# Two groups of products cut at 432 and 256 columns, and a modulation shift summed on TensorE for every feature tile

## The chip, the cores and the metric

The kernel runs on one core of one Trainium2 chip. The metric is the time of one execution on the device, in microseconds (us). Engines are named PE (TensorE, the matrix engine; PEld is its loading of weights), DVE (VectorE), ACT (ScalarE), POOL (GpSimd) and SP (SyncE, whose queue issues the transfers).

## The reference

The reference is a transformer of two layers over 512 latent tokens (`x`) and 256 context tokens (`ctx`) of 1024 features, in float32. Only the beginning of layer 0 matters here. A conditioning vector, one for the latents and one for the context, is passed through silu and multiplied by `ada_w`, which gives six modulation parts; the first two are a shift and a scale:

```
m_lat = split(silu(c) @ ada_w[l] + ada_b[l], 6)
m_ctx = split(silu(c_ctx) @ ada_w[l] + ada_b[l], 6)
u_lat = x * (1 + m_lat[1]) + m_lat[0]
u_ctx = h * (1 + m_ctx[1]) + m_ctx[0]
p_lat, p_ctx = u_lat @ w_in, u_ctx @ w_in
```

The columns of `w_in` are queries, keys, values and gates of a gated linear attention (4 heads with values of 128) and queries, keys and values of a windowed attention. Behind the mixers come an output projection, LayerNorm and an MLP, and then the second layer with a recurrent mixer and a latent attention.

## The kernel before

All 768 tokens stay on the chip. Activations lie as [feature in tile, feature tile, token], with 8 feature tiles of 128. To keep float32 accuracy, each operand of the large products is split into a high and a low part (`split`: ACT casts, DVE subtracts), and each product is made in three passes (high x high, high x low, low x high).

The part around the change is the first 170 us:

1. `ada_first` makes silu of the conditioning, and spreads it over all partitions (`scb`).
2. `in0` is a generator: each step loads, for one feature tile, the weights of the scale (`scraw`, 512 KB, three buffers), those of the shift (`shraw`, 512 KB, two buffers) and the tile of tokens (`x`, 384 KB, three buffers), in this order on the SP queue. It sums scale and shift for both streams, adds the bias, and makes the activation on ACT (`u` at L450 and its high part `acthi` at L451), and the low part `actlo` on DVE (L452). The scale is always summed on DVE by `ada_dot` (L391: weights times the spread activation, summed along the free axis). The shift is summed on PE for the tiles named in `SHP` (0, 1, 3, 5, 7; L440, eight products of two columns into PSUM), and by `ada_dot` for tiles 2, 4 and 6.
3. `proj_moving(0, ...)` takes those tiles as they come: with 128 tokens stationary, it multiplies by `VM` = 344 columns of weights (L472 to L474), for 6 token tiles and 8 feature tiles, into six PSUM banks. Its weights (`wraw`) come two feature tiles at a time, 2 x 344 columns. `ev0` copies out the gate inputs (48 columns), the values of the windowed attention (128) and the first part of the values `vt` of the gated heads (168).
4. Nine blocks of outputs are then projected with weights stationary (`dense`, L343 to L347), in parts of 512 and 256 tokens. Beside them DVE makes further modulation parts (`ada_chunk`, `araw`, L391 again); for keys and queries of the windowed attention there is a rotation by position (`rp` at L918 on PE, L920 to L922 on DVE).
5. `proj_moving(1, ...)` makes the other 344 columns, all of them `vt`, copied by `ev1`. Then come the output gates, and the gated heads, whose first product on PE is `z` at L507.

The order of the instructions of each engine is written by a scheduler, which takes what is ready by its own model of the durations, first by program order (or a priority given by `prio`), so work of later steps can fill gaps of earlier ones. On the chip, each engine and the SP queue go through this order as written.

Of the kernel before, what the change touches and what calls it, by code (L numbers as in the profile page):

```python
# [16 lines left out]
P = 128  # L17
# [33 lines left out]
SHP = (0, 1, 3, 5, 7)  # L51
PARTS = ((0, 512), (512, 256))
GH = 4
VM = 344
# [9 lines left out]
def _blocks(w):  # L64
    """[K, M] -> [M/128, 128 (k in tile), K/128, 128 (m in block)]"""
    k, m = w.shape
    return np.ascontiguousarray(w.reshape(k // P, P, m // P, P).transpose(2, 1, 0, 3))
# [18 lines left out]
def _rope_perm(half, reps):  # L86
    """lhsT of the signed swap: out[j] = sum_p m[p, j] x[p]; x1 rows get -x2, x2 rows get x1."""
    nf = half // 2
    d = 2 * half
    m = np.zeros((d * reps, d * reps), np.float32)  # L90
    for r in range(reps):
        for b in (0, half):
            for i in range(nf):
                a, c = r * d + b + i, r * d + b + nf + i
                m[c, a] = -1.0
                m[a, c] = 1.0
    return m


class Pack:  # L100
    """columns of one [128, n] array, found by name"""
# [16 lines left out]
def prepare(i):  # L118
# [19 lines left out]
    # shape-only constants  # L138
# [20 lines left out]
    # modulation weights  # L159
    aw = i['ada_w']  # L160
    def outer(w):
        """[D, D] -> [128 (output in tile), tile, inner dimension]"""
        return w.reshape(D, KT, P).transpose(2, 1, 0)
    sh = [outer(aw[0][:, :D])[:, k] if k not in SHP else _blocks(aw[0][:, k * P:(k + 1) * P])[0].reshape(P, D) for k in range(KT)]
    a['ada_sh'] = np.ascontiguousarray(np.stack(sh))
# [3 lines left out]
    # layer 0 mixer  # L169
# [6 lines left out]
    a['w0_m'] = np.ascontiguousarray(mv.reshape(KT, P, 2, VM).transpose(2, 1, 0, 3))  # L176
    a['w0_o'] = _blocks(i['ab_w_out'][0])
    # layer 1 mixer
# [54 lines left out]
def blocks(*ws):  # L233
    """the weights of each block of outputs, from parts of the inner dimension"""
    return [tuple(w[d].rearrange("p k m -> p (k m)") for w in ws) for d in range(KT)]


class Act:
    """activations [128, KT, tokens], a tile for each part of the tokens; a slice of the tokens lies in one part"""
# [17 lines left out]
class Build:  # L257
# [6 lines left out]
    @contextmanager  # L264
    def prio(self, d):
        """what is issued inside stands d instructions later (earlier, if negative) in the scheduler's order"""
# [36 lines left out]
    def psum(self, b, s=0, **more):  # L303
        """PSUM as b single banks and s pairs of banks; more: banks of other tags. Tiles of a tag start in program
        order, so streams that run side by side have tags of their own"""
# [14 lines left out]
    def split(self, raw, hi, lo, eng=None):  # L320
        """raw = hi + lo exactly, both as float32r"""
# [3 lines left out]
    def weights(self, src, n=1024, keep=None, lead=PW):  # L325
        """one [128, n] block of weights from DRAM (or two halves of one), split"""
# [12 lines left out]
    def mm3(self, whi, wlo, ahi, alo, first, last, outs):  # L339
        """outs: list of (psum, slice of the moving operand); one k tile in three passes"""  # L340
# [8 lines left out]
    def dense(self, whi, wlo, hi, lo, nk, parts=PARTS):  # L349
        """[128 out, tokens] += w^T act; w [128, nk*128]; returns one psum tile per part"""  # L350
# [9 lines left out]
    def ada_first(self, pool, m0):  # L360
        """silu of the conditioning on all partitions, [128, stream, inner dimension]"""
# [25 lines left out]
    def ada_dot(self, pool, raw, ws, out):  # L387
        """out(w) = the weights [128, inner dimension] times the activation of stream w; raw is overwritten"""
# [4 lines left out]
    def ada_chunk(self, pool, l, j, among=False):  # L393
        """modulation part j of layer l, a tile of 128 outputs at a time: the weights with the inner dimension on
        the free axis, multiplied by the activation on all partitions and summed"""
# [26 lines left out]
    def in0(self, m0, hi, lo):  # L422
        """x * (1 + scale) + shift, split, tile after tile of the features"""
# [5 lines left out]
        for k in range(KT):  # L429
# [7 lines left out]
            if k in SHP:  # L437
                sh = self.bank("sh", "n")[:, 0:2]
                for q in range(KT):
                    nc.tensor.matmul(sh, rb[:, q * P:(q + 1) * P], self.sc[:, q], start=(q == 0), stop=(q == KT - 1))  # L440
            self.ada_dot(m0, ra, (0, 1), lambda w: m[:, 1, w:w + 1])
            if k not in SHP:
                self.ada_dot(m0, rb, (0, 1), lambda w: m[:, 0, w:w + 1])
                sh = m[:, 0]
# [10 lines left out]
    def proj_moving(self, g, hi, lo, evac, feed=None):  # L455
        """[tokens, VM] = u w with the tokens stationary; feed: makes the tiles of u one after the other"""
        nc = self.nc
        outs = [self.bank("mv") for _ in range(TT)]
        for k2 in range(KT // 2):
            for _ in range(FEED if feed and k2 == 0 else 0):  # L460
                next(feed, None)
            whi, wlo = self.weights(self.a['w0_m'][g, :, 2 * k2:2 * k2 + 2].rearrange("p k m -> p (k m)"), 2 * VM,
                                    lead=0 if feed else PW)
            for kk in range(2):
# [3 lines left out]
                wh, wl = whi[:, kk * VM:(kk + 1) * VM], wlo[:, kk * VM:(kk + 1) * VM]  # L468
                for t in range(TT):
                    uh, ul = hi[:, k, t * P:(t + 1) * P], lo[:, k, t * P:(t + 1) * P]  # L470
                    o = outs[t][:, :VM]
# [3 lines left out]
        for t in range(TT):  # L475
            evac(t, outs[t][:, :VM])

    def sigmoid(self, out, src, tmp):
        """1 / (1 + exp(-src)), all on ACT within one table set"""
# [5 lines left out]
    def gla_setup(self, m0):  # L485
        """operands of each level of halved blocks, with zeros where a side has none"""
# [11 lines left out]
    def gla_head(self, m0, mx_, h, qd, kd, vt, a1T, g):  # L498
        """decays, decayed queries and keys, chunk states of one head, into g[h]"""
        nc = self.nc  # L500
        HALF = (slice(0, 64), slice(64, 128))
        # log decays (times 16): rows 0-63 forward, rows 64-127 backward shifted by one token
# [25 lines left out]
        # exponents of the middles of the chunks  # L528
# [16 lines left out]
        # state contributions of each chunk  # L545
# [25 lines left out]
    def gla_levels(self, cs, lev, W, wm, qd, kd):  # L571
        """operands of the pairs within the chunks cs, by halving blocks; a level's products two levels behind
        its exponentials"""
# [27 lines left out]
        def second(b, Dt):  # L601
# [4 lines left out]
            if b == 1:  # L606
                # neighbours and the token itself (twice, once for each direction)
# [23 lines left out]
    def gla_window(self, m0, h, cs, lev, qt, vh, S, og, hi, lo):  # L631
        """outputs of the chunks cs from the level operands and the states; normed, gated, split"""
# [48 lines left out]
    def gla(self, m0, setup, g, qd, kd, og, hi, lo):  # L681
        """all heads, in windows of two chunks: levels of the next window beside the products of this one. Those of the first are there"""
# [28 lines left out]
    def gqa(self, m0, mx_, queries, KS, K2, vg, hi, lo):  # L711
        """grouped-query attention, head by head. The scores with the queries on the partitions give each query's
        maximum; it is three more rows (exact bfloat16 parts) of the product with the keys on the partitions. The
        queries are [hi; lo] over 128 partitions against [hi; hi] of the keys, then hi against lo. Columns of
        ones beside the values give the sums, and the sink's weight is added to those."""
# [135 lines left out]
    def mixer0(self):  # L851
# [3 lines left out]
        with tc.tile_pool(name="m0", bufs=1, side="right", reuse_waits="tile") as m0, ExitStack() as m0_, \  # L855
# [15 lines left out]
            def ev0(t, o):  # L871
                nc.scalar.copy(at[:, t], o[:, 0:48])
                nc.scalar.copy(vg[:, t, 1::2], o[:, 48:176].rearrange("p (i d) -> p i d", i=2))
                nc.scalar.copy(vt[:, t, 0:VM - 176], o[:, 176:VM])

            def ev1(t, o):
                nc.scalar.copy(vt[:, t, VM - 176:512], o)
# [3 lines left out]
            with tc.tile_pool(name="ma", bufs=1, reuse_waits="tile") as ma:  # L881
# [27 lines left out]
                # grouped-query attention projections, with rope on the latent tokens  # L909
# [25 lines left out]
            # gates of the GLA heads, and the decays of the first one  # L935
# [27 lines left out]
            with tc.tile_pool(name="mb", bufs=1, reuse_waits="tile") as mb:  # L963
# [11 lines left out]
                def queries(i):  # L975
                    """parts of two heads' queries: [hi; lo] of the even head, [lo; hi] of the odd one"""
# [16 lines left out]
    def project(self, ws, hi, lo, z, g, l, parts, sums, norm, keep=None, kept=(), lead=PW):  # L993
        """z += gate * (w^T act), one part of the tokens after the other; sums collects z over the blocks. The
        norm of a part runs beside the products of the next; returns that of the last part. ws: for each block,
# [1034 lines left out]
```

## Time and profile before

| | |
|---|---|
| median of 3 runs | 2121.8 us (2116.98 to 2125.74) |
| span of the profiled execution, first to last instruction | 2106.9 us |
| PE busy | 1976.5 us, 94% |
| DVE busy | 1391.4 us, 66% |
| ACT busy | 952.7 us, 45% |
| POOL busy | 308.6 us, 15% |

The runs time the whole execution, the span only what lies between the first and the last instruction; no time of the profiled execution other than its span is given. Busy shares are means over stages with different limits; matmuls are pipelined, so that PE's busy time overlaps itself.

### The profile page before, as it was taken

Reading aid. Unit: us, or ns where it says so; the run is one execution under the profiler, and the core shown is the slowest. Engines: PE = TensorE matmul, PEld = TensorE weight load, DVE = VectorE, ACT = ScalarE, POOL = GpSimd, SP = SyncE. Lnnn points to the kernel's source line nnn. Section 1 sums busy time; section 2 is a strip of 40 time slices with the busy share of each in tenths; the row PEclk is TensorE's granted clock in tenths of the full one; section 3 lists DMA queues with packets and bytes.
Section 4 is the critical chain, followed back from the end, with each engine's and each line's share of the span. In section 5 each row is a group of like instructions: output and inputs, shape, how many; then the busy total and the mean of one; then the engine's idle time right before and its main releaser. Section 6 shows DMA issues by size and latency. Waiting matters only on the chain. (4 is left out here: it accounts for less than half of the span.)

```text
span 2106.9 us, 35640 instructions
## 1 busy us (share of the span) xinstructions
PE 1976.5 (94%) x14304; PEld 1643.3 (78%) x14304; DVE 1391.4 (66%) x2574; ACT 952.7 (45%) x1835; POOL 308.6 (15%) x517
## 2 busy tenths in 40 slices
PE   8998999989899999999989999978888899999998
PEld 6877666667788888888878877767677797888887
DVE  8775898736897656534484558878887555444454
ACT  5426676544622222222255646765654535333332
POOL 0003455301200000000021020033342011000001
PEclk9999799999999999999999999998999899999999
DMA  8650000053354554312243100000001412332241
GB/s 298 202 161 14 1 2 1 1 180 102 114 183 134 158 160 145 117 60 93 88 150 113 41 1 6 9 9 2 3 2 33 132 59 85 108 103 90 90 136 41
DMA packets 66282, 180.38 MB, mean 86 GB/s; under 512 B 7235, under 2 KB 12099, under 8 KB 65989
## 3 DMA queue, kind: packets, MB, share of 16 engines
q1 hardware_dynamic: 66116, 178.11, 26.4%
q8 instruction: 112, 1.84, 0.4%
q14 instruction: 54, 0.43, 0.1%
HBM read 172.57 MB, written 5.51 MB: 85 GB/s over the span
## 5 line engine op out<-in xcount | busy, mean ns | idle before, releaser
L322 ACT CAST whi<-wraw 128x1024 fp32r<-128x1024 f32 (+2 forms) x253 | 221.4, 878 | 641.2 <-PE mm L345 565.8
L343 PE MATMUL mm<-acthi,whi 128*128 128x512 f32 (+1 forms) x1464 | 443.4, 349 | 12.9 <-ACT whi L322 12.2
L347 PE MATMUL mm<-acthi,wlo 128*128 128x512 f32 (+1 forms) x1464 | 438.9, 346 | 9.3 <-DVE wlo L323 9.2
L345 PE MATMUL mm<-actlo,whi 128*128 128x512 f32 (+1 forms) x1464 | 442.2, 348 | 2.6 <-POOL actlo L1085 2.5
L323 DVE TENSOR_TENSOR wlo<-wraw,whi 128x1024 fp32r<-128x1024 f32 (+2 forms) x253 | 257.1, 1019 | 218.6 <-ACT whi L322 214.2
L343 PEld LDWEIGHTS mm<-acthi,whi 128*128 128x128 f32 x1464 | 250.7, 191 | 51.3 <-ACT whi L322 14.9
L347 PEld LDWEIGHTS mm<-acthi,wlo 128*128 128x128 f32 x1464 | 251.4, 192 | 49.0 <-DVE wlo L323 13.2
L345 PEld LDWEIGHTS mm<-actlo,whi 128*128 128x128 f32 x1464 | 251.0, 191 | 39.8 <-POOL actlo L1085 3.9
L347 PE MATMUL mm<-hh,wlo 128*128 128x512 f32 (+1 forms) x832 | 252.8, 341 | 3.6 <-DVE wlo L323 3.6
L343 PE MATMUL mm<-hh,whi 128*128 128x512 f32 (+1 forms) x832 | 253.7, 342 | 0.0
L345 PE MATMUL mm<-hl,whi 128*128 128x512 f32 (+1 forms) x832 | 253.3, 342 | 0.1
L1085 POOL TENSOR_TENSOR actlo<-lnu,acthi 128x256 fp32r<-128x256 f32 (+1 forms) x48 | 60.3, 1271 | 717.4 <-DVE lnu L1083 630.4
L347 PEld LDWEIGHTS mm<-hh,wlo 128*128 128x128 f32 x832 | 143.9, 189 | 23.2 <-DVE wlo L323 4.2
L345 PEld LDWEIGHTS mm<-hl,whi 128*128 128x128 f32 x832 | 143.6, 189 | 19.2 <-issue 0.7
L343 PEld LDWEIGHTS mm<-hh,whi 128*128 128x128 f32 x832 | 143.1, 189 | 19.5 <-issue 1.0
L1157 DVE SCALAR_TENSOR_TENSOR z<-mm,mod,z 128x512 f32<-128x512 f32 (+1 forms) x144 | 94.0, 659 | 96.6 <-PE mm L347 96.3
L391 DVE SCALAR_TENSOR_TENSOR araw<-araw,scb 128x1024 f32<-128x1024 f32 x80 | 97.8, 1222 | 56.4 <-DMA araw<-in_ada_r_dram 55.6
L1011 DVE SCALAR_TENSOR_TENSOR z<-mm,mod,z 128x256 f32<-128x256 f32 (+1 forms) x64 | 34.9, 548 | 81.2 <-PE mm L347 79.6
L322 ACT CAST hh<-relu 128x512 fp32r<-128x512 f32 (+1 forms) x100 | 50.4, 534 | 79.5 <-DVE relu L1109 79.5
L615 POOL TENSOR_TENSOR lk<-kd,Dt 64x128 f32<-64x128 f32 x144 | 74.5, 517 | 48.5 <-ACT Dt L597 20.0
L323 DVE TENSOR_TENSOR hl<-relu,hh 128x512 fp32r<-128x512 f32 (+1 forms) x100 | 56.1, 587 | 26.5 <-ACT hh L322 26.1
L391 DVE SCALAR_TENSOR_TENSOR aprod<-araw,scb 128x1024 bf16<-128x1024 f32 x48 | 58.5, 1220 | 19.6 <-DMA araw<-in_ada_r_dram 19.6
(465 smaller groups left out, 3394.0 us busy)
## 6 DMA issues: line engine op xcount, KB each, us to landing
araw<-in_ada_r_dram SPq DMA_DIRECT2D x80, 512.0 KB, 3.8
wraw<-in_w_dram SPq DMA_DIRECT2D x72, 512.0 KB, 3.5
wraw<-in_w_dram SPq DMA_DIRECT2D x144, 256.0 KB, 2.6
wraw<-in_w_s_dram SPq DMA_DIRECT2D x31, 512.0 KB, 3.6
wraw<-in_w_o_dram SPq DMA_DIRECT2D x22, 512.0 KB, 3.6
scraw<-in_ada_sc_dram SPq DMA_DIRECT2D x8, 512.0 KB, 5.3
shraw<-in_ada_sh_dram SPq DMA_DIRECT2D x8, 512.0 KB, 5.7
x<-in_xT_dram SPq DMA_DIRECT2D x8, 384.0 KB, 5.7
```

The costliest lines, as they stand in the source:

```text
L322: self.nc.scalar.copy(hi, raw)
L323: (eng or self.nc.vector).tensor_tensor(lo, raw, hi.bitcast(F32), op=ALU.subtract)
L343: mm(o, whi, ahi[:, sl], start=first, stop=False)
L345: mm(o, whi, alo[:, sl], start=False, stop=False)
L347: mm(o, wlo, ahi[:, sl], start=False, stop=last)
L391: self.nc.vector.scalar_tensor_tensor(pr, raw, 1.0, self.scb[:, w], op0=ALU.mult, op1=ALU.mult, accum_out=out(w))
L615: nc.gpsimd.tensor_tensor(K[r, :, x], kk[r, :, x], d[r, :, x], op=ALU.mult)
L1011: nc.vector.scalar_tensor_tensor(zs, o, self.mod[:, l, self.wh(i, parts), g, d:d + 1], zs, op0=ALU.mult, op1=ALU.add)
L1085: eng.tensor_tensor(lo[:, k, sl], u, hi[:, k, sl].bitcast(F32), op=ALU.subtract)
L1157: nc.vector.scalar_tensor_tensor(z[:, d, sl], o, self.mod[:, l, self.wh(i, parts), 5, d:d + 1], z[:, d, sl], op0=ALU.mult, op1=ALU.add)
```

## The change

Tiles 2, 4 and 6 have their shift summed on PE like the others, and `SHP` goes; the shift's weights are laid out as blocks for all tiles. The first group of products has 432 columns (gate inputs, windowed values, and the values of two gated heads), the second has 256 (the values of the other two heads). Comments and docstrings that the diff also takes out are left out here.

```diff
-SHP = (0, 1, 3, 5, 7)
-VM = 344
+VM = 432, 256
...
-    sh = [outer(aw[0][:, :D])[:, k] if k not in SHP else _blocks(aw[0][:, k * P:(k + 1) * P])[0].reshape(P, D) for k in range(KT)]
-    a['ada_sh'] = np.ascontiguousarray(np.stack(sh))
+    a['ada_sh'] = _blocks(aw[0][:, :D]).reshape(KT, P, D)
...
-    a['w0_m'] = np.ascontiguousarray(mv.reshape(KT, P, 2, VM).transpose(2, 1, 0, 3))
+    for g, m in enumerate((mv[:, :VM[0]], mv[:, VM[0]:])):
+        a[f'w0_m{g}'] = np.ascontiguousarray(m.reshape(KT, P, VM[g]).transpose(1, 0, 2))
...
-            if k in SHP:
-                sh = self.bank("sh", "n")[:, 0:2]
-                for q in range(KT):
-                    nc.tensor.matmul(sh, rb[:, q * P:(q + 1) * P], self.sc[:, q], start=(q == 0), stop=(q == KT - 1))
+            sh = self.bank("sh", "n")[:, 0:2]
+            for q in range(KT):
+                nc.tensor.matmul(sh, rb[:, q * P:(q + 1) * P], self.sc[:, q], start=(q == 0), stop=(q == KT - 1))
             self.ada_dot(m0, ra, (0, 1), lambda w: m[:, 1, w:w + 1])
-            if k not in SHP:
-                self.ada_dot(m0, rb, (0, 1), lambda w: m[:, 0, w:w + 1])
-                sh = m[:, 0]
...
+        vm = VM[g]
-            whi, wlo = self.weights(self.a['w0_m'][g, :, 2 * k2:2 * k2 + 2].rearrange("p k m -> p (k m)"), 2 * VM,
+            whi, wlo = self.weights(self.a[f'w0_m{g}'][:, 2 * k2:2 * k2 + 2].rearrange("p k m -> p (k m)"), 2 * vm,
...
-                wh, wl = whi[:, kk * VM:(kk + 1) * VM], wlo[:, kk * VM:(kk + 1) * VM]
+                wh, wl = whi[:, kk * vm:(kk + 1) * vm], wlo[:, kk * vm:(kk + 1) * vm]
...
-                    o = outs[t][:, :VM]
+                    o = outs[t][:, :vm]
...
-                nc.scalar.copy(vt[:, t, 0:VM - 176], o[:, 176:VM])
+                nc.scalar.copy(vt[:, t, 0:256], o[:, 176:432])
...
-                nc.scalar.copy(vt[:, t, VM - 176:512], o)
+                nc.scalar.copy(vt[:, t, 256:512], o)
```

## Rows read from the trace of the kernel before

**Rows 1.** The page: its first line.

```profile
span 2106.9 us, 35640 instructions
```

**Rows 2.** Stages of 10 us: start:end, length, busy us (instructions) of each engine, granted clock, DMA share, GB/s.

```profile
20.00:30.00 10.00, 9.66 (x67) 9.38 (x65) 10.00 (x22) 5.68 (x9) 0.00 (x0) 1.00 0.84 294
30.00:40.00 10.00, 7.90 (x41) 6.79 (x40) 10.00 (x22) 5.66 (x9) 0.00 (x0) 0.83 0.94 342
...
110.00:120.00 10.00, 7.74 (x25) 5.90 (x26) 8.54 (x17) 2.44 (x4) 0.00 (x0) 0.66 0.46 136
...
200.00:210.00 10.00, 3.96 (x27) 2.93 (x26) 8.03 (x20) 8.11 (x22) 7.28 (x23) 0.85 0.04 15
```

**Rows 3.** Waits, 0 to 53 us: waited for: us in total, times, longest.

```profile
PE mv L472 <- ACT acthi L451: 5.1, 4, 2.1
```

**Rows 4.** Timeline of PE and its weight loads: start, us, engine, line, operation [idle before].

```profile
10.69 3.63 PE L440 MATMUL sh<-scc,shraw 128*128 128x2 f32 x32
...
15.18 0.42 PE L472 MATMUL mv<-whi,acthi 128*128 128x344 f32 x1 [0.86 <-ACT acthi L451]
...
21.00 1.84 PE L440 MATMUL sh<-scc,shraw 128*128 128x2 f32 x16
...
30.76 1.86 PEld L440 LDWEIGHTS sh<-scc,shraw 128*128 128x128 f32 x16 [0.25 <-DMA shraw<-in_ada_sh_dram]
...
52.58 0.38 PE L895 MATMUL a1t<-col,at 128*48 128x128 f32 x2
...
112.26 2.08 PE L918 MATMUL rp<-qg,rope 128*128 128x512 f32 x2 [4.15 <-ACT qg L915]
...
140.34 0.32 PE L472 MATMUL mv<-whi,acthi 128*128 128x344 f32 x1
...
163.84 0.51 PE L343 MATMUL mm<-acthi,whi 128*128 128x512 f32 x2
...
172.41 1.56 PE L507 MATMUL z<-a1T,con 48*128 48x512 f32 x4
```

**Rows 5.** Timeline of DVE at tile 2: dot products, shift and then scale.

```profile
19.73 1.21 DVE L391 SCALAR_TENSOR_TENSOR aprod<-shraw,scb 128x1024 bf16<-128x1024 f32 x1
...
22.15 1.21 DVE L391 SCALAR_TENSOR_TENSOR aprod<-scraw,scb 128x1024 bf16<-128x1024 f32 x1
```

**Rows 6.** Timeline of PE: pairs of 512 and 256 columns; 256 columns alone.

```profile
99.28 0.51 PE L345 MATMUL mm<-actlo,whi 128*128 128x512 f32 x2
...
106.91 0.51 PE L347 MATMUL mm<-acthi,wlo 128*128 128x512 f32 x2
...
1680.01 0.28 PE L345 MATMUL mm<-actlo,whi 128*128 128x256 f32 x1
...
1681.81 0.28 PE L345 MATMUL mm<-actlo,whi 128*128 128x256 f32 x1
```

**Rows 7.** Stages of 1 us, columns as in rows 2.

```profile
16.00:17.00 1.00, 1.00 (x4) 0.86 (x4) 1.00 (x3) 1.00 (x3) 0.00 (x0) 0.50 1.03 410
...
38.00:39.00 1.00, 1.00 (x5) 1.00 (x5) 1.00 (x2) 0.55 (x2) 0.00 (x0) 0.50 1.06 426
```

**Rows 8.** Groups by line, 0 to 55 us: count | busy us, mean ns | idle before.

```profile
L322 ACT CAST whi<-wraw 128x688 fp32r<-128x688 f32 x4 | 3.1, 768 | 14.8 <-DMA wraw<-in_w_m_dram 14.8
```

**Rows 9.** Timeline of DVE and of ACT ahead of the hole on PE.

```profile
99.84 1.23 DVE L391 SCALAR_TENSOR_TENSOR aprod<-araw,scb 128x1024 bf16<-128x1024 f32 x1 [0.82 <-DMA araw<-in_ada_r_dram]
...
102.13 0.68 DVE L920 TENSOR_TENSOR ropet<-rp,rope 128x512 f32<-128x512 f32 x1
...
105.25 1.70 ACT L926 CAST ks<-kg 64x768 fp32r<-64x768 f32 x2 [7.75 <-DVE kg L922]
...
109.59 1.04 ACT L322 CAST whi<-wraw 128x1024 fp32r<-128x1024 f32 x1
```

**Rows 10.** Timeline of the SP queue: a load of shift weights.

```profile
22.87 0.33 SPq L433 DMA_DIRECT2D shraw<-in_ada_sh_dram  x1
```

**Rows 11.** The tile of the shift's weights, 0 to 52 us: its loads.

```profile
DMA to landing us min/median/max: 4.0/5.7/8.0
```

More of the change, by code (lines that the diff above doesn't have):

```diff
@@ L475, in proj_moving @@
         for t in range(TT):
-            evac(t, outs[t][:, :VM])
+            evac(t, outs[t][:, :vm])
     def sigmoid(self, out, src, tmp):
```

## The prediction

> **What bounds the kernel now.** I read the page first: the profiled span is 2106.9 us [rows 1]. The runs have a median of 2121.8 us, 14.9 us more, which I take as what lies around the span; the sum below is made against 2106.9 and 14.9 is put back at the end. Then I read the table of stages, because both edits lie in the first 170 us. From 20 to 40 us the reader is to see VectorE at 10.00 us of 10 while PE has 9.66 and 7.90 [rows 2]: here VectorE sets the pace. One pair of feature tiles takes 10 us: the shift sums of two pairs begin on PE at 21.00 and, with their weight loads, at 30.76 [rows 4]. The waits of this stage say the same from the other side: PE stood 5.1 us in front of the moving products until ScalarE had made the high parts of the activations [rows 3], and those wait for the scale and shift that VectorE sums.
>
> PE's own timeline shows the stage from end to end: the first shift sums start at 10.69, the stage ends at 52.58 with the first transpose, so it takes 41.9 us, and behind it the projections run [rows 4]. The second group of products runs from 140.34 to 163.84 without a gap [rows 4]; there PE sets the pace. Between the two lies one hole of 4.15 us, which ends at 112.26 [rows 4], and from 110 to 120 us the mean granted clock is 0.66 [rows 2].
>
> **The shift.** For feature tiles 2, 4 and 6 VectorE now makes two dot products over 1024 elements each. The first starts at 19.73 and the next work follows at 22.15, so 2.42 us per tile are taken off VectorE [rows 5], 7.3 us in all. The small addition that follows stays, it only reads PSUM. PE gets 16 instructions for each of the three tiles, 1.84 us a tile [rows 4]: 5.5 us more.
>
> **The products.** Group 0 grows by 88 columns, group 1 shrinks by 88, each in 144 matmuls (8 feature tiles, 6 token tiles, 3 passes). The trace has 256-column matmuls that follow each other every 0.120 us (15 steps in 1.80 us) and 22 pairs of 512 and 256 columns in 7.63 us, 0.347 a pair [rows 6]; so 512 columns take 0.227, and a column costs 0.107/256 = 0.416 ns. By this line 344 columns take 0.1566 and 432 take 0.1932. Check: group 1 took 23.5 us, with a rope product in its midst, 0.163 each, so the line isn't high. An instruction changes by 36.6 ns, a group by 144 x 36.6 ns = 5.3 us (6.2 if all of 0.163 came down to 0.120; I take the line, since the rope product stays). Group 1 gains 5.3 us where PE has no gap, so all of it moves what stands behind: also the first product of the gated heads at 172.41 [rows 4], with which the next stage begins.
>
> **The first stage anew.** It was bound by VectorE; per pair of tiles the three candidates now are:
> - VectorE: 10.0 less 2.4, plus at most 0.2 for the wider low part: 7.8 us.
> - PE: 36 products of 0.1932 and two shift sums of 1.84: 7.0 + 3.7 = 10.6 us.
> - Transfers: 2 x (512 + 512 + 384) + 432 KB are 3.3 MB; at the 410 to 426 GB/s of the busy microseconds [rows 7] 8.0 us.
>
> So PE becomes the bound, at 10.6 us instead of 10.0. Now the whole stage. Before, its 41.9 us are five shift sums (9.2), 144 products at 0.157 (22.6), waits for the activations (5.1), two stretches of some 3.2 us at half clock, near 16 and 38 us [rows 7], which cost half of themselves (3.2), and 1.8 of small gaps. After: eight shift sums 14.7; products 27.8; the wait before the first product, 0.86 at 15.18 [rows 4], which nothing removes; the first slow stretch, 1.6; the other waits and the second slow stretch go, since PE has no idle time in front of it any more. That is 45.0, plus small gaps between 0 and 1.8. I take half, 0.9: 45.9 us, 4.0 more than before (bounds +3.1 and +4.9).
>
> **Small things.** The first group's casts grow from 688 to 864 columns; a 688-column cast takes 768 ns [rows 8], in proportion 0.2 us more, four times, on ScalarE, which has 5.7 us of 10 busy [rows 2]; the second group gives it back. The bytes only move from one group to the other. If that cover went, 0.8 us would be the price. The shift weights are laid out in another order with the same size, and the issue count is the same.
>
> The Trainium skill (DMA: Bandwidth & Descriptors, section "Where 436 GB/s comes from") sets the limit for loads from HBM at about 358 GB/s. This trace does not agree: it shows 410 to 426. By the page the pair's transfers would take 9.3 us, still under PE's 10.6, but with half the slack for the late shift weights of the second rival.
>
> **The sum.** +4.0 in the first stage, -5.3 in the second group: -1.3 us. 2106.9 - 1.3 + 14.9 = 2120.5 us. The two edits work against each other: the shift takes VectorE out of the way, and the room so made is filled by the columns and by the shift sums themselves.
>
> **Rivals.** *The hole at 108 us closes (faster).* The hole has this chain: VectorE stood before a dot product of the modulation until its weights had landed, at 99.84, so the rope of the keys came only at 102.13; ScalarE waited for it until 105.25, and behind its copies the cast of the next weights came at 109.59 [rows 9]. PE stood 4.15 us [rows 4] and came back at half clock: the mean of 0.66 from 110 to 120 [rows 2] is 6.8 us at half, of which some 5.7 lie behind PE's return and cost half of themselves, 2.9; 7 us in all. After the change VectorE is done with the first stage some 3 us earlier and PE 4 later, so VectorE has a lead. For: the hole, 4.15 us, is shorter than this lead of 7. Against: VectorE's order is written by a planner that sees the lead too and may put more dot products ahead of the rope, each late by its transfer as now; then the hole grows by about 1 us. Time if it closes: 2120.5 - 7 = 2113.5 us.
>
> *PE waits in its order (slower).* A shift buffer (there are two) is loaded anew only when its sum is made: the load for tile 4 is issued at 22.87 [rows 10], behind the dot products of tile 2, and a load lands 4.0 to 8.0 us after its issue, 5.7 in the median [rows 11]. If the shift sums of a pair stand in PE's order ahead of the products that should cover this, each pair takes 5.7 + 3.7 + 7.0 = 16.4 us instead of 10.6, with three such pairs 17 us more, and PE comes back at half clock each time, 1.6 us apiece, 22 us together. Against: the sum of tile 5 waited only 0.25 us for its load [rows 4]; for: that it waited at all shows that its load is hardly earlier than its turn, and now twice as many sums stand in the order. The Trainium skill (TensorE: Matmul & The Clock Gate, section "Step-by-step: what each phase is for") says that matmuls stay in program order and only weight loads are pulled ahead; no row here shows a product that overtakes a sum. It turns the sign against the forecast when more than 1.3 us are lost, and makes the kernel measurably slower from 12 us on; at 16 of the 22 us the time is 2136 us.
>
> *The planner draws the rest anew.* Everything behind is ordered by the same planner from its own durations; two changed sizes at the start can shift which of the small operations of the gated heads goes first, where PE has only 3.96 of 10 us [rows 2]. Either sign, some 12 us; I see somewhat more room for gain, since VectorE has 7 us less to do. 2108 or 2133 us.
>
> *The shift's edit does nothing:* if VectorE or the transfers still set the pace at 10 us a pair, the stage would stay at 41.9 us and group 1's gain would be whole: 2116.5 us. PE's 10.6 speaks against it; I leave it within the forecast's band.
>
> **Chances and range.** A measurement of this kernel can tell about 0.5% from no change, 10.6 us. The forecast (2116 to 2125): 0.46, all of it within 0.5%. The hole closes: 0.20, of it 0.06 beyond 0.5%. PE waits in order: 0.14, of it 0.11 slower by more. The planner: 0.20, of it 0.11 faster, 0.06 the same, 0.03 slower. Together faster 0.17, the same 0.69, slower 0.14. The range of 8 in 10 reaches over the closed hole to 2109 on one side and to half of the waits on the other, 2131.
>
> **What would show it.** VectorE has no dot product on the shift weights any more and is below 9 of 10 us between 20 and 40; PE is at 10 of 10 there; PE's first transpose of the stage comes at 56 to 57 instead of 52.58; the second group takes 17.3 to 18 us; its last product ends near 162.5 if the hole is as it was. The prediction is wrong if PE stands before a shift sum for more than 2 us in all, if its clock falls in the first stage more than once, or if the hole changes by more than 3 us.

## The result, and the profile after

| | before | after |
|---|---|---|
| median of the runs | 2121.8 us (7 runs) | 2131.45 us (7 runs, 2124.51 to 2139.05) |
| ratio to before | 1 | 1.0063, 95% interval 1.0043 to 1.0083 |
| span of the profiled execution | 2106.9 us | 2136.1 us |

By the ratio the kernel became 13 us slower (the two medians are 9.7 us apart). The forecast was 2120.5 us with a range to 2131; the time lies just beyond that end, on the side that had a chance of 0.14. In the runs that came later a profiled execution took 1.8 us more than its span (2125.97 against 2124.2 in the second profile of before), so the 14.9 us that the prediction put around the span are not there: the first profiled execution of before was some 13 us quicker than its median. The difference of the two spans, 29 us, therefore says too much; the stages are what can be compared. The profiled execution of after is the second slowest of its seven (2137.86 us) and has the lowest mean clock of them (0.952, the others 0.953 to 0.959), so it is one of the longer executions.

Line numbers after the change are 4 lower in this part (L440 is L438, L472 to L474 are L468 to L470, L322 is L321). First the timeline of PE through the first stage and on to the gated heads (start, us, engine, line, operation, idle before), which answers to [rows 4]:

```profile
11.09 4.75 PE L438 MATMUL sh<-scc,shraw 128*128 128x2 f32 x32
...
17.24 0.73 PE L469 MATMUL mv<-wlo,acthi 128*128 128x432 f32 x1 [0.84 <-DVE wlo L322]
17.77 3.41 PE L438 MATMUL sh<-scc,shraw 128*128 128x2 f32 x16
...
27.27 1.84 PE L438 MATMUL sh<-scc,shraw 128*128 128x2 f32 x16
...
40.59 1.84 PE L438 MATMUL sh<-scc,shraw 128*128 128x2 f32 x16
...
46.27 0.73 PE L468 MATMUL mv<-whi,acthi 128*128 128x432 f32 x1 [3.14 <-ACT whi L321]
46.80 3.41 PE L438 MATMUL sh<-scc,shraw 128*128 128x2 f32 x16
...
61.21 1.44 PE L468 MATMUL mv<-whi,acthi 128*128 128x432 f32 x6 [0.25 <-ACT whi L321]
...
68.36 0.38 PE L891 MATMUL a1t<-col,at 128*48 128x128 f32 x2
...
129.11 1.60 PE L914 MATMUL rp<-qg,rope 128*128 128x512 f32 x2 [4.77 <-ACT qg L911]
...
155.51 0.28 PE L468 MATMUL mv<-whi,acthi 128*128 128x256 f32 x1
...
173.81 0.52 PE L342 MATMUL mm<-acthi,whi 128*128 128x512 f32 x2
...
182.38 1.56 PE L503 MATMUL z<-a1T,con 48*128 48x512 f32 x4
```

The stage now runs from 11.09 to 68.36, 57.3 us instead of 41.9: its first transpose comes 15.8 us later. The same sixteen instructions of a shift sum take 1.84 us in one place and 3.41 us in another. The hole is still there, 4.77 us for 4.15. The second group takes 18.3 us (155.51 to 173.81) instead of 23.5, so the first product of the heads, `z`, comes 10.0 us later.

Then the stages of 10 us of the kernel after (columns as in [rows 2]):

```profile
10.00:20.00 10.00, 9.16 (x49) 7.80 (x47) 8.65 (x18) 7.23 (x11) 0.00 (x0) 0.68 0.88 330
20.00:30.00 10.00, 10.00 (x44) 9.49 (x45) 3.61 (x10) 3.30 (x5) 0.00 (x0) 0.64 0.70 274
30.00:40.00 10.00, 10.00 (x60) 9.70 (x59) 8.88 (x18) 5.01 (x8) 0.00 (x0) 1.00 0.75 266
40.00:50.00 10.00, 6.86 (x40) 6.44 (x40) 5.21 (x12) 3.30 (x5) 0.00 (x0) 0.71 0.80 280
50.00:60.00 10.00, 10.00 (x48) 9.52 (x49) 4.62 (x11) 4.66 (x8) 0.00 (x0) 0.77 0.08 31
```

VectorE went from 10.00 to 3.61 in the stage from 20 us, and PE is at 10.00: PE sets the pace, as forecast. But the granted clock is what the reader is to see. It has two levels, 2.4 GHz (1.00) and 1.2 GHz (0.50), so a mean of 0.68 is (1 - 0.68) x 20 = 6.4 us at the lower one; then come 7.2, 0, 5.8 and 4.6 us, 24 us in all. From 20 to 30 PE was busy throughout and still issued 44 matmuls where it had issued 67; those were narrower (344 columns), which is a part of the difference.

Last, the waits from 0 to 69 us (who, for what: total, times, longest), which answer to [rows 3]:

```profile
ACT u L445 <- issue: 22.0, 5, 6.7
DVE ss L440 <- PE sh L438: 14.7, 6, 6.4
...
PE mv L468 <- ACT whi L321: 3.4, 2, 3.1
...
PE mv L469 <- DVE wlo L322: 0.8, 1, 0.8
```

No shift sum waits for its load. PE's wait for the activations is gone; in its place VectorE waits 14.7 us for PE's sums, and PE 3.1 us for a cast of weights. That cast can be followed in the timelines of VectorE and ScalarE:

```profile
42.48 0.22 DVE L440 TENSOR_SCALAR ss<-sh,ssb 128x2 f32<-128x2 f32 x1 [1.91 <-PE sh L438]
```

```profile
42.91 0.81 ACT L445 ACTIVATE u<-x,ss 128x512 f32<-128x512 f32 x1 [3.57 <-issue]
...
44.84 0.58 ACT L446 ACTIVATE acthi<-x,ss 128x256 fp32r<-128x256 f32 x1
45.33 0.89 ACT L321 CAST whi<-wraw 128x864 fp32r<-128x864 f32 x1
```

It stands in ScalarE's order behind four activations, these wait for the shift, and the shift waits for PE's sum of 40.59. So PE waits for a cast that waits for PE.

### The profile page after: what moved, and what is told of

The parts are those of the page before. It is cut to its first block, busy times and chain, and to the rows that moved or that the text cites. A ratio compares the mean times of both kernels' runs of the same rounds, so it can differ in the third digit from the quotient of the medians.

```text
span 2136.1 us, 35722 instructions
## 1 busy us (share of the span) xinstructions
PE 2003.7 (94%) x14352; PEld 1663.3 (78%) x14352; DVE 1386.2 (65%) x2562; ACT 953.9 (45%) x1835; POOL 307.4 (14%) x517
## 3 DMA queue, kind: packets, MB, share of 16 engines
q8 instruction: 112, 1.84, 0.4%
## 5 line engine op out<-in xcount | busy, mean ns | idle before, releaser
L321 ACT CAST whi<-wraw 128x1024 fp32r<-128x1024 f32 (+2 forms) x253 | 221.4, 878 | 632.4 <-PE mm L344 552.1
L322 DVE TENSOR_TENSOR wlo<-wraw,whi 128x1024 fp32r<-128x1024 f32 (+2 forms) x253 | 258.8, 1026 | 220.9 <-ACT whi L321 216.5
L321 ACT CAST hh<-relu 128x512 fp32r<-128x512 f32 (+1 forms) x100 | 50.5, 534 | 75.1 <-DVE relu L1105 75.1
L322 DVE TENSOR_TENSOR hl<-relu,hh 128x512 fp32r<-128x512 f32 (+1 forms) x100 | 56.2, 588 | 26.5 <-ACT hh L321 26.1
```

The source lines that it names most:

```text
L321: self.nc.scalar.copy(hi, raw)
L322: (eng or self.nc.vector).tensor_tensor(lo, raw, hi.bitcast(F32), op=ALU.subtract)
```

## The experiments

Sixteen kernels were run, each timed beside the kernel before on the same chip. In the expectations A is that the thin shift sums (two columns) bring PE's granted clock down, which lengthens them and the products behind them; B that the loss is one of order (casts behind activations that wait for a sum); C that it is only the added work; D that the wider products lose by themselves; G and H belong to the gated heads and are told there.

| run | ratio to before (95%) | first transpose | first `z` |
|---|---|---|---|
| after | 1.0063 (1.0043 to 1.0083) | 68.4 | 182.4 |
| c1_before: before again | 1.0000 (0.9981 to 1.0019) | 54.7 | 175.7 |
| e1_groups | 1.0002 (0.9983 to 1.0021) | 53.8 | 167.9 |
| e2_shift | 1.0047 (1.0029 to 1.0065) | 63.6 | 183.3 |
| e4_wide | 1.0029 (1.0012 to 1.0045) | 60.7 | 173.7 |
| e5_lead | 1.0054 (1.0031 to 1.0076) | 70.0 | 185.6 |
| e6_before_wide | 1.0014 (0.9993 to 1.0035) | 56.6 | 175.6 |
| e7_groups_wide | 1.0004 (0.9983 to 1.0025) | 54.5 | 167.8 |
| e8_512_wide | 1.0014 (0.9998 to 1.0029) | 60.7 | 172.6 |

**The two edits apart.** The groups alone:

```diff
-VM = 344
+VM = 432, 256
```

> Only the groups of 432 and 256 columns; the shift stays on VectorE for tiles 2, 4 and 6. Theory A (the shift sums bring TensorE's clock down, and with it the first stage) and theory B (the sums stand in TensorE's order, and activations and casts wait behind them): the first stage, 52.6 us before and 68.4 after the change, ends at 53 to 56, the second group is 5.3 us shorter, the kernel is 2 to 5 us faster than before. Rival D (the wider products themselves fill the stage): it ends at 60 or later, the kernel is 2 us or more slower than before.

The shift alone:

```diff
-SHP = (0, 1, 3, 5, 7)
+SHP = (0, 1, 2, 3, 4, 5, 6, 7)
```

> Only the shift on TensorE for all tiles; groups of 344 and 344. A and B: the first stage ends at 60 to 66 us, more than 6 us are spent at half clock, the kernel is 8 to 14 us slower than before. Rival C (only the added work counts: 5.5 us more, in a stage in which TensorE idled 5.1 us and lost 3.2 at half clock): it ends at 52 to 55, the kernel is within 2 us of before.

The shift alone costs 10 us by the ratio (11 by the medians, 2130.47 against 2119.37), most of what the whole change costs; the groups alone cost nothing and gain nothing, which ends D. The stage of e2 ends at 63.6 with unchanged products, 9 us later than in the second profile of before; three more sums are 5.5 us of work, so in this profile C falls short (all runs follow below). The timeline of PE in e2 shows the same two things as after:

```profile
17.79 3.41 PE L440 MATMUL sh<-scc,shraw 128*128 128x2 f32 x16
...
43.44 0.65 PE L472 MATMUL mv<-whi,acthi 128*128 128x344 f32 x1 [3.69 <-ACT whi L322]
43.89 3.40 PE L440 MATMUL sh<-scc,shraw 128*128 128x2 f32 x16
```

In e1 the wider products ran with a clock of 1.00 from 20 to 50 us, and PE still waited for activations, 0.78 and 0.89 us: there VectorE keeps the pace.

**The width of the sums.** The whole change, with 64 columns per sum, of which 62 are ones and are not read:

```diff
+        self.scw = m0.tile([P, KT, SW], F32, name="scw")
+        nc.gpsimd.memset(self.scw, 1.0)
+        nc.vector.tensor_copy(self.scw[:, :, 0:2], self.sc)
...
-            sh = self.bank("sh", "n")[:, 0:2]
+            sh = self.bank("sh", "n")[:, 0:SW]
...
-                nc.tensor.matmul(sh, rb[:, q * P:(q + 1) * P], self.sc[:, q], start=(q == 0), stop=(q == KT - 1))
+                nc.tensor.matmul(sh, rb[:, q * P:(q + 1) * P], self.scw[:, q], start=(q == 0), stop=(q == KT - 1))
+            sh = sh[:, 0:2]
```

> The changed kernel with the shift sums 64 columns wide instead of 2 (62 of them ones, their results not read): TensorE does more in the same instructions. A: the two long stretches at half clock (13 and 10 us) shrink by half or more, the first stage ends at 57 to 62 us, the kernel is 6 to 11 us faster than the changed one. B: the clock goes as it did, the stage ends at 66 to 70, the same time as the changed kernel.

The stages of e4, and below them its timeline of PE:

```profile
10.00:20.00 10.00, 9.25 (x59) 7.45 (x59) 9.21 (x18) 7.23 (x11) 0.00 (x0) 1.00 0.78 295
20.00:30.00 10.00, 10.00 (x62) 9.72 (x62) 9.29 (x21) 5.93 (x9) 0.00 (x0) 1.00 1.02 382
30.00:40.00 10.00, 8.06 (x53) 7.51 (x52) 5.37 (x12) 5.41 (x9) 0.00 (x0) 1.00 0.87 312
40.00:50.00 10.00, 9.54 (x54) 9.25 (x55) 6.83 (x16) 2.92 (x5) 0.00 (x0) 0.83 0.46 177
```

```profile
11.87 3.68 PE L442 MATMUL sh<-scw,shraw 128*128 128x64 f32 x32
...
17.65 1.90 PE L442 MATMUL sh<-scw,shraw 128*128 128x64 f32 x16
...
40.46 0.66 PE L473 MATMUL mv<-whi,acthi 128*128 128x432 f32 x2 [2.40 <-ACT whi L322]
40.96 2.35 PE L442 MATMUL sh<-scw,shraw 128*128 128x64 f32 x16
```

A sum of 64 columns takes 1.90 us where one of 2 takes 1.84, so the width itself is nearly free. In after the clock fell within the first two sums, which took 4.75 us; the same two, which come first in both kernels, take 3.68 here. The clock stays at 1.00 up to 40 us, the third sum no longer takes 3.41, and the stage ends 7.7 us earlier. The half clock that is left comes behind the wait of 2.40 us for the cast. This is A, for the slow stretch that begins at the first sums; the wait for the cast is B's and stays. The edit also moved the planner's order a little: five products stand ahead of the third sum, in after two. That alone isn't the cause, for in e5, further down, eight stand there and the clock falls as in after.

The kernel e10, which differs from e4 only in the gated heads, gives a second profile of this stage. It ends at 61.4:

```profile
10.00:20.00 10.00, 9.14 (x63) 8.11 (x64) 9.96 (x21) 6.97 (x11) 0.00 (x0) 1.00 0.90 337
20.00:30.00 10.00, 10.00 (x67) 9.76 (x65) 8.26 (x18) 5.82 (x9) 0.00 (x0) 1.00 1.03 404
```

The same width in the kernel before, in the groups alone, and with the groups at 512 and 176:

> The kernel before with its five shift sums 64 columns wide (only the first two columns are read). A: the slow stretch behind the first sums goes, the first stage ends at 49 to 52 us instead of 52.6, the kernel is 1 to 4 us faster than before. Rival C (thin sums cost only their own time): it ends at 52.6 to 54.

> Groups of 432 and 256, the shift of five tiles on TensorE with sums 64 columns wide. A: the first stage ends at 51 to 53 us (53.8 with thin sums), the first product of the gated heads comes 5 to 7 us earlier than before, the kernel is 3 to 7 us faster than before. If something behind that product gives back what the groups win (the median of the groups alone did not move), it is within 2 us of before.

> As the run before, with groups of 512 and 176 columns. TensorE then has 10.0 us of work per pair of tiles, as much as VectorE: the first stage ends at 53 to 57, the second group is 4.8 us shorter again if a 176-column product follows the line of 0.416 ns a column, 0 to 3 us shorter if the loading of its stationary operand bounds it; against the run before between 3 us faster and 2 us slower.

None of the three is faster than before. Where VectorE sets the pace, with five sums, wide ones gain nothing (first transpose at 56.6 and 54.5 against 54.7 and 53.8), and they don't hold the clock either. Two stages of e6:

```profile
20.00:30.00 10.00, 7.64 (x43) 7.40 (x42) 10.00 (x22) 5.66 (x9) 0.00 (x0) 0.76 0.87 308
...
40.00:50.00 10.00, 5.64 (x35) 4.95 (x34) 8.70 (x19) 3.63 (x6) 0.00 (x0) 0.78 0.85 310
```

The first stage of every kernel can be set beside the others, with the time at half clock summed from 10 to 70 us as above (c2 to c5 and e9 to e14 come further down; their edits lie in the heads):

| sums on PE | us at half clock in the first stage, a profile each |
|---|---|
| five of 2 columns | before 6.8, c1 13.8, c2 10.4, c4 6.8, c5 10.2; e1 3.4, e9 3.4, e11 7.0, e13 10.2, e14 6.8 |
| five of 64 columns | e6 13.6, e7 3.4, e8 6.8 |
| eight of 2 columns | after 24.0, e5 24.0, e2 20.4 |
| eight of 64 columns | e4 3.4, e10 6.8 |

With five sums the width makes no difference that stands out from one profile to the next; with eight it does. So A's price is shown for eight thin sums on a PE that sets the pace, and what A was expected to give elsewhere didn't come.

At 512 columns the first stage grows by 6 us and `z` comes 4.8 us later than with 432. The second group takes 17.6 us there, 0.7 less than with 256 columns: products of 176 columns follow each other every 0.113 us, where the prediction's line would give 0.087.

**The order of the casts.** The whole change, with the weights of the first group ahead of the activations in the order, by as much as elsewhere in the kernel:

```diff
-                                    lead=0 if feed else PW)
+                                    lead=PL if feed else PW)
```

> The changed kernel with the weights of the first group ahead of their place in the order (a lead of 50 instead of 0), so that their casts no longer stand behind activations that wait for a shift sum. B: the waits of 0.8 and 3.1 us for these casts go, the first stage ends at 58 to 64 us, the kernel is 4 to 10 us faster than the changed one. A alone: the sums are as many and as thin, the stretches at half clock stay within 3 us of the 23 us they had, the stage ends at 64 to 68.

```profile
10.00:20.00 10.00, 10.00 (x50) 8.81 (x49) 8.64 (x19) 6.88 (x11) 0.00 (x0) 0.68 0.89 325
20.00:30.00 10.00, 10.00 (x39) 9.50 (x40) 5.05 (x11) 2.74 (x5) 0.00 (x0) 0.63 0.83 314
```

```profile
64.74 0.73 PE L468 MATMUL mv<-whi,acthi 128*128 128x432 f32 x1 [4.45 <-ACT acthi L446]
```

Stages and the timeline of PE of e5. Both expectations missed the end of the stage, which comes at 70.0. The wait of 3.14 us went, a wait of 4.45 us for activations came, the clock is as low as in after in the first 20 us, and the half clock of the stage is 24.0 us again. As a remedy the order fails; the clock's part is the same with another order, which is what A says.

**All runs.** A profile is one execution, but the mean clock of every run is on record. (1 - clock) x span is then the time that half clock costs if PE is busy in it, and the rest is the span as it would be at full clock; both in us, means of the runs:

| | runs | (1 - clock) x span | rest |
|---|---|---|---|
| before, beside e1 to e5 | 30 | 84.6 | 2033.1 |
| e1_groups | 12 | 88.3 | 2029.7 |
| e2_shift | 12 | 86.9 | 2040.3 |
| e4_wide | 12 | 87.5 | 2036.9 |
| e5_lead | 8 | 90.0 | 2038.7 |
| after | 7 | 92.5 | 2037.5 |

Of the 12 us between after and before, 8 are half clock (standard error 2.6) and 4 are the rest; after ran at another time than the others. Between after and e4, 5 are half clock (2.9) and 0.6 are the rest (1.6), which fits A. In e2 it is the other way round: 2 of 9.5 us are half clock (2.0) and 7 the rest (1.0). So for the shift alone, C's added work and the waits are most of the price, and its one profile gives the clock too large a part.

**A second profile of before**, to see how far two executions of one kernel differ:

> The kernel before, unchanged, profiled a second time. If the 3.5 to 8 us that every variant so far shows between the first product of the gated heads and the end of that stage belong to the one profiled execution of before, this profile shows them too (its span is 2113 us or more, the stage before it ends at 52 to 54). If they belong to the changes, the profile stays within 3 us of the first one there.

Its span is 2124.2 us, 17 us over the first one's, with the same medians. Its `z` comes 3.3 us later, the rest lies behind. Its first stage has 13.8 us at half clock where the first profile has 6.8. So a few us of a single profile are no evidence, in the first stage or behind it; the 20 to 24 us of eight thin sums stand above all of these.

**Where the 5 us of the groups go.** In e1 the first `z` comes 7.8 us earlier than in c1_before, and yet the time doesn't move. From `z` on PE's order of instructions is the same in before, the groups alone, the shift alone and after, and the waits of PE there are the same to 0.1 us where they are longest (6.0 and 4.3 us). The stretch from the first `z` to the last `U` of the heads, in c1_before, in e1 and in after (columns as in [rows 2]):

```profile
175.70:353.90 178.20, 164.24 (x938) 118.27 (x938) 147.69 (x375) 124.10 (x343) 91.20 (x176) 0.88 0.01 2
```

```profile
167.90:352.90 185.00, 170.72 (x939) 122.30 (x939) 147.84 (x378) 124.86 (x345) 91.28 (x177) 0.84 0.01 2
```

```profile
182.40:366.10 183.70, 169.68 (x938) 121.44 (x938) 147.38 (x377) 124.31 (x343) 90.90 (x176) 0.84 0.01 2
```

Idle time on PE is 14.0, 14.3 and 14.0 us. What differs is PE's busy time over the same instructions, and it differs by the clock: a mean of 0.88 over 178.2 us is a loss of 0.12 x 178.2 = 21.4 us, 0.84 of 185.0 one of 29.6, and after has 29.4. So in these executions the 7 us are given back to a longer half clock. As a trait of the groups this isn't shown: over all runs, what e1, e9, e7, e14 and e13 lose to half clock in the whole execution differs from before with the same other edit by +3.7, -2.6, -0.4, +1.3 and -5.3 us (standard errors near 2), and single runs of before lose between 72 and 98 us. G says that this half clock begins with PE's wait of 6.0 us and would go with it, H that other engines set the length of this stage whatever PE does. The first try put six products (128x512, constants, overwritten) ahead of the base product that waits:

```diff
+            if h == 0 and cs == (4, 5) and j == 0:
+                for _ in range(6):
+                    mm(base, self.c('ident', 0, P), self.k('a2', 0, 512), start=True, stop=True)
             mm(base[:, 0:P], bl(lk[64], 0, P), bl(lq[64], 0, P), start=True, stop=False)
```

> Leaves nothing out and adds six products (128x512, a constant by a constant, result overwritten) on PE just ahead of the first window's base product, where PE idles for 6.0 us in the gated heads and the granted clock falls to 0.50 for about 35 us. The kernel before otherwise. Theory G (the idle stretch brings the half clock, and the half clock is what sets the length of this stage, since PE's order and its waits there are the same in every kernel): the time lost to half clock between the first z and the last U falls from 19 to 21 us to under 10, the first 6 us of wait go, and the time falls by 8 to 17 us, to 2102 to 2112. Rival H (the small products that follow bring the clock down by themselves): the stretch stays at 0.50 and the time is within 4 us of 2121.

> The groups of 432 and 256 alone, with the same six added products. Theory G: the 7.8 us by which this kernel reaches the first z earlier than the kernel before were given back to a longer half clock (30 us lost against 21); with the clock held, both lose the same there, and this kernel ends 5 to 8 us ahead of the kernel before with the added products, 2096 to 2106. Rival H: no hold, the gain stays given back, and the two are within 3 us of each other near 2120.

> The whole change with shift sums 64 columns wide (60 of them not read), with the same six added products. Theory G: 5 to 17 us under the same kernel without them (2125.8), 2109 to 2120. Rival H: 2122 to 2130.

> The groups of 432 and 256 alone, with the six products and eight more (128x256) ahead of the window's last output product, where PE waits 4.3 us for DVE. If the first filler is enough by itself, the second only adds PE time that was idle: within 3 us of the kernel with the first alone. If the second wait brings the half clock by itself, this one is the faster by 4 us or more.

The products waited themselves. The waits of PE in e9:

```profile
PE base L654 <- DVE og L960: 5.9, 1, 5.9
```

The profile names VectorE's `og` here and a memory clear on POOL in before; constants need neither, so what PE waits for is the PSUM bank that `og` still reads. The fillers became added work: c2 1.0034 (1.0014 to 1.0055), e9 0.9996 (0.9980 to 1.0011), e10 1.0030 (1.0015 to 1.0046), e11 0.9992 (0.9971 to 1.0013). The expected times of G were missed. The mean clock from `z` to the last `U` is 0.87 in c2 and in e9, and there e9 ends 5.6 us ahead (2119.16 against 2124.73), as G expected of two kernels with the same loss. But e11 speaks against G. It has eight more products ahead of the last output product, where PE waits 4.3 us, and it does hold the clock; its stretch from `z` to the last `U`:

```profile
170.20:350.20 180.00, 167.90 (x966) 120.06 (x966) 149.38 (x375) 124.05 (x343) 92.01 (x176) 0.92 0.01 2
```

Over its 12 runs (1 - clock) x span is 15 us less than in e1 (73.2 against 88.3, standard error 2.3), and yet its median is only 2 us lower (2117.58 against 2119.63). The added products are an estimated 4.6 us of work by [rows 6] (12 instructions of 512 columns at 0.227, 16 of 256 at 0.120), so more than half of what was won from the clock did not shorten the kernel. That bears out H.

Then the bank was changed, in c5 (before) and e14 (groups), and in c4 and e13 the fillers went into a bank of the scores, with the eight products ahead of the last output product as in e11. What c5 and e14 change:

```diff
             self.psum(PG[0], u=PG[1], q=PG[2], qo=PG[3])
+            self.bank("first", "q")
+            self.bank("first", "q")
```

> The kernel before, with the two banks of the queries' scores handed out first at the change of PSUM in the gated heads, so that the first window's base product gets another bank than the one that the last dense product left for DVE. Nothing else changes and PE's order is the same. Theory G: the wait of 6.0 us ahead of the base product shrinks to under 3 us, the granted clock stays at 1.00 for longer there, the time lost to half clock falls from about 20 to under 14 us, and the time falls by 4 to 12 us, to 2107 to 2115. Theory H (DVE, ACT and POOL set the length of the stage): the wait only moves to the next product that needs them, and the time is within 4 us of 2119.

> The groups of 432 and 256 alone, with the same order of banks. Theory G: it loses as much to half clock in the heads as the kernel before with that order, within 3 us, so it ends 4 to 8 us ahead of it, 2100 to 2110. Theory H: it ends within 3 us of it.

> The kernel before, with six products of 128x512 (constants, not read) into a bank of the scores ahead of the base product, and eight of 128x256 ahead of the window's last output product, where PE waits 4.3 us. Theory G: PE is busy through both waits, the time lost to half clock from the first z to the last U falls under 12 us, and the time falls to 2106 to 2116. Theory H: the clock holds, but the stage is no shorter than 173 us, and the time is within 4 us of 2119.

> The groups of 432 and 256 alone, with the same products in both waits. Theory G: 4 to 8 us ahead of the kernel before with them, 2099 to 2111. Theory H: within 3 us of it.

The waits of PE in c5, and the timeline of PE in e13:

```profile
PE o L644 <- DVE A L662: 4.3, 1, 4.3
PE z L507 <- DVE og L955: 2.7, 1, 2.7
PE gsc L745 <- POOL q L736: 1.7, 1, 1.7
PE base L654 <- POOL zerob L967: 1.6, 1, 1.6
```

```profile
199.46 5.32 PE L655 MATMUL fill<-con,col 128*128 128x512 f32 x12
205.65 0.46 PE L656 MATMUL base<-lq,lk 128*128 128x128 f32 x2 [0.88 <-POOL mE L731]
...
218.72 0.80 PE L656 MATMUL base<-lq,lk 128*128 128x128 f32 x2 [5.00 <-ACT A L662]
...
227.38 4.95 PE L675 MATMUL o<-con,col 128*128 128x256 f32 x16
```

With the other bank the wait of 6.0 us splits into 1.6, 2.7 and 1.7 and PE falls to half clock all the same (a mean of 0.86 from `z` to the last `U` in c5). With fillers in both places the first wait is covered, and a new one of 5.0 us for ScalarE comes behind it. Times: c5 1.0016 (0.9994 to 1.0038), e14 1.0000 (0.9981 to 1.0018), c4 1.0029 (1.0008 to 1.0050), e13 1.0004 (0.9983 to 1.0025). G's remedy fails, and that speaks for H too: take a wait from PE here, and the next one comes from another engine. The groups against before with the same other edit: +0.3, -5.6, +1.2, -2.4 and -3.4 us between the medians (e1, e9, e7, e14, e13). So the groups are worth some 2 us (2.8 by the means of the runs, standard error 0.9), less than their 5.2 us of PE time. No version beats the kernel before by more than the measurement can tell.

## Why the prediction was wrong

- **The first stage anew failed**: 57.3 us where the sum gave 45.9. The step that failed is "the other waits and the second slow stretch go, since PE has no idle time in front of it any more". Terms of work were right: eight sums of 1.84 us are 14.7, 144 products at 0.193 are 27.8, and e4 and after show both durations at full clock. Idle time is 0.84 + 3.14 + 0.25 = 4.2 us where 1.8 stood in the sum, and the rest, 57.3 - 14.7 - 27.8 - 4.2 = 10.6 us, is the price of 24 us of half clock; the sum had 1.6. Both slow stretches were mis-sized: the first, 3.2 us at half clock in the sum, lasted 13.6 us (10 to 30 us), and the second, which was to go, 10.4 us (40 to 60 us). The prediction took a busy PE for a PE at full clock. PE was busy all through 20 to 30 us, at 0.64. One of its own signs of being wrong came: the clock fell in the first stage more than once. It was a weak sign, since it falls twice in both profiles of before.
- **The half clock is shown** by e4 and e10: there the sums are wide and all else is as in after but for the planner's small shift, and the first slow stretch went in both (3.4 and 6.8 us at half clock in the stage instead of 24), with 7.7 and 7.0 us gained in the stage; the ratio of e4 to before is 1.0029 where after has 1.0063, which is 7 us of 2120 (5.6 between the medians). The rest of the stage's excess is the added work, the wait for the cast and the half clock behind it.
- **The rival "PE waits in its order" had the sign, and half of the mechanism.** That the time went its way is in the main luck, since the clock did most of it. PE did come to wait on its own sums, but not by the loads of the shift weights: no sum waited for one. The loop goes over VectorE's addition, ScalarE's activations and the cast behind them, 3.1 us, once.
- **The pace**: right. VectorE is off the path and PE is at 10 of 10 us from 20 to 40 us.
- **The second group**: right, 5.2 us for 5.3. 256 columns step every 0.120 us (155.51, 155.63, ...), as the two rows [rows 6] said.
- **The hole**: 4.77 us for 4.15, within the 3 us allowed; the rival that it closes failed. PE's delay shrank behind it, from 16.85 us at the end of the hole to 15.17 at the start of the second group; the clock from 130 to 140 us has a mean of 0.85, where before it was 0.66 behind the hole [rows 2], which fits.
- **The whole**, against c1_before, whose span is nearer to the medians: 13.7 us late at the first transpose (68.4 and 54.7), 6.7 at `z`, 12.2 at the last `U` (366.1 and 353.9), 11.9 at the end of the span; the ratio says 13.
- **The time around the span**: 1.8 us, not 14.9. It cancelled in the forecast, which set a difference on the median.

What stays open: what makes the clock stay low longer in the heads in one execution than in another. With one order of instructions, and the same waits to 0.1 us in all but e4 (one of 7.2 instead of 4.3) and c5 and e14 (other banks), the loss there by the mean clock is 19 us in before, 21 in c1_before and e6, 25 or 26 in c5 and e4, and 27 to 30 in e2, e7, e5, e14, after, e8 and e1. Neither the time at which `z` begins (172.4 in before, 172.6 in e8) nor a longer wait tells them apart. Over all runs e7 and e8 lose as much as before in the whole execution (84.8 and 86.4 against 85.0), so much of this is the one execution that was profiled. Open as well is why eight thin sums bring the clock down for so long and five don't; the runs show that the width matters, not how.

## What to carry to other kernels

An engine that becomes the bound is costed at the clock that it will be granted with its new mix of instructions, not at the duration that the same instruction had between waits: here eight thin sums cost twice, once as work and once for what they slowed. Before work is moved to PE to relieve VectorE, follow the loop back: does PE's next operand hang, over two other engines' orders, on the moved work? And a gain in a stage in the middle of a kernel counts only when the next stage starts from it; here PE's saving of 5 us was in full at `z` and was mostly gone 180 us later. Where single executions differ by some us, look at several, and at the mean clock of all runs, before a difference is given a cause.

## What the runs showed of the hardware

- A product of fp32 with 64 columns takes as long as one with 2: 1.90 and 1.84 us for a chain of eight (sixteen records), and 3.41 us at the lower clock. With eight such sums in the first stage, PE was at the lower clock for 20 to 24 us when they were thin (three profiles) and for 3 to 7 us when they were wide (two); with five of them the width made no such difference.
- The clock fell to 0.50 while PE showed 10.00 us of 10 busy (20 to 30 us after): the busy share doesn't tell the clock.
- Where a product waits for several things, the engine named was not the cause: the 6.0 us named after POOL stayed as 5.9 us for products of constants in the same bank, and split when the bank was another.
- Moving products of 176 columns follow each other every 0.113 us (e8) and of 256 columns every 0.120 us, so the last 80 columns cost 0.007 us, where from 256 to 512 a column costs 0.4 ns [rows 6].
- The mean granted clock of one kernel over 30 to 35 runs lies between 0.954 and 0.966 (before), which is 72 to 98 us of a span of 2117 by (1 - clock) x span.
